# A four-mixer hybrid layer on one core: matmuls regrouped in the recurrent mixers, masks added once a bank, and attention products of two key tiles put together

## The chip, the cores and the metric

One core of one Trainium2 chip runs the whole program. The metric is the device time of one execution in microseconds, and the comparison is between medians of several executions. The engines are TensorE (PE for matmuls, PEld for weight loads), VectorE (DVE), ScalarE (ACT), GpSimd (POOL) and SyncE (SP), which issues most of the DMAs.

## The reference

Two layers over 1024 tokens of width 1024. Each layer projects the tokens into four groups of four heads of 64, mixes each group in another way, gates, projects back, adds to the scaled input and normalises:

```python
def hybrid_mixer(x, w_in, b_in, ...):
    cols = split_cols(jnp.einsum('btd,dn->btn', x, w_in) + b_in)
    # A: attention over a window of 128 keys, with a sink
    y_a = flat(banded_attention(q_a, k_a, heads(cols['a_v']), A_WINDOW, a_sinks)) * silu(cols['a_z'])
    # B: mLSTM in chunks of 128
    h_b = mlstm_chunkwise(q, k, v, i_pre, f_pre)
    y_b = sigmoid(cols['b_o']) * flat(h_b) * silu(cols['b_z'])
    # C: HGRN2, a gated recurrence
    o_c = hgrn2_chunkwise(heads(silu(cols['c_q'])), heads(log(f_c)), heads(1.0 - f_c), heads(cols['c_i']))
    y_c = flat(normed(o_c)) * silu(cols['c_z'])
    # D: compressed keys + 8 selected blocks of 64 + a window of 512
    o_d = nsa_attention(q_d, ...)
    y_d = flat(o_d) * silu(cols['d_z'])
    return jnp.einsum('btm,md->btd', concatenate([y_a, y_b, y_c, y_d], -1), w_out)

def reference(x, ...):
    h = layer_norm(x, ln0_g, ln0_b)
    for l in range(2):
        y = hybrid_mixer(h, ...)
        h = layer_norm(DN_ALPHA * h + y, ln_g[l], ln_b[l])
    return h
```

In the mLSTM of a chunk, with `b` the running sum of the log forget gates and `m` a running maximum:

```python
D = where(causal, b[t] - b[s] + i[s], -inf)
m_t = maximum(max(D, -1), b + m)
S = einsum('htd,hsd->hts', q, k) * exp(D - m_t)
num = S @ v + exp(b + m - m_t) * (q @ C)
```

## The kernel before, in words

The program is unrolled in Python. A stage is one half of the sequence (512 tokens, four tiles of 128) in one layer, so there are four stages. In each stage the four groups run in the order D, C, A, B. A group first makes its projections (`proj_tok`, `proj_feat`: fp32r matmuls of a high and a low part, three for each product) and then loops over its four tiles ("mix"). The driver at the end of the file runs one tile of the current group, then one projection of the next, and so on, so that projections stand between the mixers' matmuls. Within this order a scheduler fixes each engine's instruction order ahead of the run; the engines wait for each other by semaphores. Weights come as pieces by SP's DMA queue (`load_piece`), are rounded to a high part on ScalarE (L266), and POOL makes the low part (L267).

The pieces that the change touches:

- `scores` (L354) makes attention scores for one query tile. The keys are cut into one or two cuts of at most 512; a PSUM bank holds four heads of 128 keys, two of up to 256, or one of more. For each head: two fp32r score matmuls (L377, and L381 or L379), then for the first 128 keys of a full window a mask matmul (L383) and for the last 128 keys the causal mask (L385). A mask matmul multiplies a bf16 identity with a bf16 mask of 128 columns, so that 0 or -1e30 is added. VectorE takes the maximum of a bank (L387), ScalarE the exponential (L392); then the weights are scaled (L415, L417).
- `values` (L420) transposes the weights of one key tile for four heads (L427, four transposes into `ps_pt`, one of two PSUM buffers), copies them to an SBUF tile `PT` (ScalarE at odd tiles, L430, VectorE at even ones, L432; three buffers), and multiplies with the values (L434): for each pair of heads one fp32 matmul of 256 columns, into 64 of the 128 partitions of `O`. The next key tile follows. In D the compressed product (L672) comes before, into the same `O`.
- Group C (L817 on): `front(c)` makes the decay factors (POOL L761, L762; ScalarE L767; VectorE L778), the score matmuls (L796, L801) and the masked tile `Af`. Then, for each of four heads, the product with the state `St` (L831: 64 rows, 64 columns) and the product with the values (L832: 128 rows, 64 columns); then two transposes of the keys (L836), the copy `kh` (L838), and the state's update (L843, L849). `ms` (L856) is a sum over 64 rows with two halves of the array.
- Group B: the gates of all four tiles and heads lie as rows 32c + h. VectorE scans them into `rB`, `rU`, `rM`, `rE` (L977 to L991). `front(c)` adds the causal mask (L1008, bf16 identity) and, for each head, spreads one row of `rM` over 128 partitions by an fp32 matmul of four rows with `sel` (L1012). The query-key products (L1017) share the bank `SW`. In the same way `rE` is spread into `xb` (L1032).

Of the kernel before, what the change touches and what calls it, by code (L numbers as in the profile page):

```python
# [23 lines left out]
WB, AB, PB, PTB, PER_TILE = 6, 2, 6, 3, 1  # L24
# [65 lines left out]
def consts():  # L90
    c = {}
    c['ident'] = np.eye(128, dtype=np.float32)
    q = np.arange(128)
    lo = np.where(q[None, :] <= q[:, None], 0.0, NEG)
    up = np.where(q[None, :] > q[:, None], 0.0, NEG)
    c['masks'] = np.stack([lo, up, lo.T], 1).astype(np.float32)
# [29 lines left out]
    sel = np.zeros((128, 4, 128), np.float32)  # L126
    for h in range(4):
        sel[h::32, h, :] = 1.0
    c['sel'] = sel.reshape(128, 512)
    return c  # L130
# [15 lines left out]
def tile_hybrid(ctx, tc, I, out, dbg=None, depth=DEPTH):  # L146
# [74 lines left out]
    masks = const.tile([128, 3, 128], BF16, name="masks_bf")  # L221
    cmask = const.tile([128, NT, 64], BF16, name="cmask_bf")
    identb = const.tile([128, 128], BF16, name="ident_bf")
# [4 lines left out]
    sel = const.tile([128, 512], F32, name="sel_sb")  # L228
# [4 lines left out]
    G.tensor_copy(identb, ident)  # L233

    def load_consts():

        for name, dst in (('masks', masks), ('cmask', cmask), ('lvm', lvm)):
            d2 = dst.rearrange("p a b -> p (a b)")
            n = d2.shape[1]
            m_ = mp.tile([128, 512], F32, tag="P", name="m_", bufs=PB)  # L240
            SY.dma_start(m_[:, :n], I[name] if name == 'lvm' else I[name].rearrange("p a b -> p (a b)"))
            G.tensor_copy(d2, m_[:, :n])
        for name, dst in (('rowok', rowok), ('rope_e', rope_e), ('impk', impk), ('sel', sel)):
            SY.dma_start(dst, I[name])
# [109 lines left out]
    def scores(i, k0, A1, A2, kcols, Kblk, weigh, win, sink=None, A3=None):  # L354
# [10 lines left out]
        for c, (a, b) in enumerate(cuts):  # L365
            n = b - a
            hb = 4 if n <= 128 else 2 if n <= 256 else 1
            Pc = [mp.tile([128, 2, 512], F32, tag="P", name="P", bufs=PB) for _ in range(2)]
            P.append(Pc)
            for h0 in range(0, NH, hb):  # L370
                Sp = psS.tile([128, 512], F32, tag="S", name="S_ps")[:, :hb * n].rearrange("p (h k) -> p h k", h=hb)
                for z in range(hb):
                    h = h0 + z
                    o_ = Sp[:, z, :]
                    m0, m1 = lo_mask and c == 0, b == nk * 128
                    kc_ = kcols(h, a, b)
                    PE.matmul(o_, A1[:, h, :], kc_, start=True, stop=False)  # L377
                    if Kblk is not None:
                        PE.matmul(o_, A3[:, h, :], Kblk[:, a:b], start=False, stop=not (m0 or m1))  # L379
                    else:  # L380
                        PE.matmul(o_, A2[:, h, :], kc_, start=False, stop=not (m0 or m1))  # L381
                    if m0:
                        PE.matmul(o_[:, 0:128], identb, masks[:, 1, :], start=False, stop=not m1)  # L383
                    if m1:
                        PE.matmul(o_[:, n - 128:n], identb, masks[:, 0, :], start=False, stop=True)  # L385
# [33 lines left out]

    def values(sc, Vt, O, first, last):  # L420
        k0, cuts, P = sc
        nk = cuts[-1][1] // 128
        for c, (a, b) in enumerate(cuts):
            for kb in range(a // 128, b // 128):
                ps = psT.tile([128, 4, 128], F32, tag="T", name="ps_pt")
                for h in range(NH):
                    PE.transpose(ps[:, h, :], P[c][h // 2][:, h % 2, kb * 128 - a:kb * 128 - a + 128], ident)  # L427
# [3 lines left out]
                else:  # L431
                    V.tensor_copy(PT, ps)  # L432
                for g in range(2):
                    PE.matmul(O[64 * g:64 * g + 64, :], Vt(k0 + kb, g),  # L434
                              PT[:, 2 * g:2 * g + 2, :].rearrange("p a b -> p (a b)"),
                              start=(first and kb == 0), stop=(last and kb == nk - 1))
# [3 lines left out]
    def groups(stage):  # L440
# [83 lines left out]
        def group_D():  # L524
# [86 lines left out]
            def front(t):  # L611
# [8 lines left out]
                PE.matmul(Sc3, identb, bc(cmask[:, i, :nc_], 4, 0), start=True, stop=False)  # L620
# [76 lines left out]
        def group_C():  # L697
# [121 lines left out]
            for c in range(NTH):  # L819
# [4 lines left out]
                O = psO.tile([128, 256], F32, tag="O", name="Oc")  # L824
                for ct in range(2):
                    for hh in range(2):
                        h = 2 * ct + hh
                        rows = slice(64 * hh, 64 * hh + 64)
                        o_ = O[rows, ct * 128:(ct + 1) * 128]
                        if i > 0:  # L830
                            PE.matmul(o_, St[rows, ct, :], qe[rows, ct * 128:(ct + 1) * 128], start=(ct == 0), stop=False)  # L831
                        PE.matmul(o_, Vc[:, c, 64 * h:64 * h + 64], Af[:, hh, ct, :], start=(i == 0 and ct == 0), stop=(ct == 1))  # L832
                if i < NT - 1:
# [4 lines left out]
                    S.copy(out=kh.rearrange("p a b -> p (a b)"), in_=kt_ps)  # L838
                    s_ps = psT.tile([128, 2, 64], F32, tag="T", name="s_ps")
# [73 lines left out]
        def group_B():  # L913
# [55 lines left out]
            V.tensor_tensor(lf[:, 0, :].rearrange("p (c w) -> p c w", c=4)[:, :, 0:4], l1, l0, op=OP.subtract)  # L969
            V.tensor_copy(lf[:, 1, :].rearrange("p (c w) -> p c w", c=4)[:, :, 0:4], gi[:, :, 12:16])  # L970
# [5 lines left out]
            rk = sm.tile([128, 4], F32, tag="rk", name="rk")  # L976
            V.tensor_tensor_scan(rB, ones, r_ps[:, 0, :], 0.0, op0=OP.mult, op1=OP.add)  # L977
# [4 lines left out]
            if hf == 1:  # L982
                V.tensor_copy(rk[0:4, 0:1], mcar[0:4, :])
            for c in range(NTH):
                p_ = slice(32 * c, 32 * c + 4)
                dst = rk[32 * c + 32:32 * c + 36, 0:1] if c < NTH - 1 else mcar[0:4, :]
# [4 lines left out]
            V.tensor_scalar(rE, rM, rk[:, 0:1], None, op0=OP.add)  # L991
            u_ps = psT.tile([128, 2, 128], F32, tag="T", name="u_ps")
# [9 lines left out]
            def front(c):  # L1002
                i = T0 + c
                cs_ = slice(c * 128, (c + 1) * 128)
                p_ = slice(32 * c, 32 * c + 4)
                SW = [psS.tile([128, 512], F32, tag="S", name="SW") for _ in range(2)]
                for hh in range(2):
                    PE.matmul(SW[hh][:, 0:256].rearrange("p (h t) -> p h t", h=2), identb, bc(masks[:, 2, :], 2, 0),  # L1008
                              start=True, stop=False)
                    for ct in range(2):  # L1010
                        h = 2 * ct + hh
                        PE.matmul(SW[hh][:, ct * 128:(ct + 1) * 128], sel[p_, h * 128:(h + 1) * 128], rM[p_, :],  # L1012
                                  start=False, stop=(ct == 1))
# [17 lines left out]
                for p in range(2):  # L1031
                    PE.matmul(xb[:, p, :], sel[p_, 256 * p + 64:256 * p + 192], rE[p_, :], start=True, stop=True)  # L1032
# [177 lines left out]
```

## Time and profile before

| | |
|---|---|
| median of three runs | 1646.14 us (1645.08 to 1652.29) |
| the profiled execution | 1654.33 us; span 1652.5 us |
| instructions | 29596, of them 10948 matmul records |
| granted TensorE clock, mean | 0.962 |
| DMA | 126.70 MB, mean 77 GB/s |

A row of the busy times gives the time in which an engine had an instruction, as a share of the span; TensorE's matmuls are pipelined, so that the durations of neighbours overlap and the distance between two starts says more. Rows of the order of time give the start in us from the span's start, the duration, the engine, the line, the operation, out<-in, its rows*columns in the array, then partitions x elements, and a count where equal ones follow each other. Groups give the count, the busy time, the mean duration in ns and the idle time of the engine before them.

### The profile page before, as it was taken

The page shows a single profiled execution, that of the slowest core. Times are in us where ns is not written, and L with a number is a line of the kernel's source. Part 1 is how long each engine was busy: PE and PEld are TensorE (multiplying, and loading weights), DVE is VectorE, ACT ScalarE, POOL GpSimd, SP SyncE. Part 2 cuts the span into 40 slices and gives each one's busy share as a digit, 9 for nine tenths or more (in the row PEclk, how much of TensorE's full clock was granted, in tenths as well). Part 3 has the DMA queues.
Part 4 walks back from the last instruction along what each step waited for, and adds up shares of the span by engine and source line. Part 5 has one row for each costly group of instructions (what it writes and reads, how often), then busy time and mean ns, then how long its engine had stood idle before and what let it go on. Part 6 is the DMA issues. An engine that isn't in the chain of part 4 may idle for free.

```text
span 1652.5 us, 29596 instructions
## 1 busy us (share of the span) xinstructions
PE 1538.6 (93%) x10948; PEld 1206.1 (73%) x10948; DVE 1026.2 (62%) x2454; ACT 798.3 (48%) x1865; POOL 848.7 (51%) x1173
## 2 busy tenths in 40 slices
PE   4999999899979989999998999999997999999995
PEld 3787688678767657787877768786886765688774
DVE  6256835874787776357447676456448777735737
ACT  2356535544356664455435653444434666434541
POOL 4733784546643138634575468544565321873442
PEclk9999999989989999999999999999998999799997
DMA  5322023441441001224134212233134210022311
GB/s 180 91 64 59 15 76 90 155 142 45 120 144 52 26 1 46 65 68 142 44 108 153 74 33 56 55 107 105 36 105 160 55 52 1 20 66 65 90 52 51
DMA packets 64752, 126.70 MB, mean 77 GB/s; under 512 B 10112, under 2 KB 16032, under 8 KB 64608
## 3 DMA queue, kind: packets, MB, share of 16 engines
q1 hardware_dynamic: 63744, 122.72, 25.4%
q8 instruction: 86, 1.41, 0.4%
q10 hardware_dynamic: 864, 2.10, 0.3%
q14 instruction: 58, 0.48, 0.1%
HBM read 114.30 MB, written 10.49 MB: 76 GB/s over the span
## 4 chain that ended last, share of the span: by engine, by line
PE 66%; DVE 19%; POOL 5%; issue 3%; DMA 3%; ACT 3%; SPq 0%; DVEq 0%; POOLq 0%; ACTq 0%
PE ps_f L307 7%; PE ps_f L306 6%; PE ps_f L305 6%; PE ps_p L290 5%; PE ps_p L291 4%; PE ps_p L292 4%; PE ps_pt L427 4%; PE O L434 4%; PE ps_o L478 2%; PE ps_o L476 2%; PE S_ps L377 2%; DVE QK L950 2%; PE ps_o L477 2%; PE S_ab L796 2%; DMA w_raw<-in_w_in 2%
## 5 line engine op out<-in xcount | busy, mean ns | idle before, releaser
L267 POOL TENSOR_TENSOR w_split<-w_raw,w_split 128x512 fp32r<-128x512 f32 (+2 forms) x320 | 416.0, 1307 | 380.7 <-ACT w_split L266 350.6
L266 ACT CAST w_split<-w_raw 128x512 fp32r<-128x512 f32 (+2 forms) x320 | 194.4, 611 | 238.9 <-DMA w_raw<-in_w_in 109.5
L305 PE MATMUL ps_f<-hT_hi,w_split 128*128 128x512 f32 x608 | 246.0, 405 | 0.0
L306 PE MATMUL ps_f<-hT_lo,w_split 128*128 128x512 f32 x608 | 244.0, 401 | 0.0
L307 PE MATMUL ps_f<-hT_hi,w_split 128*128 128x512 f32 x608 | 243.5, 402 | 0.0
L290 PE MATMUL ps_p<-w_split,hT_hi 128*128 128x256 f32 (+1 forms) x768 | 227.3, 298 | 8.0 <-DVE hT_lo L257 5.5
L291 PE MATMUL ps_p<-w_split,hT_hi 128*128 128x256 f32 (+1 forms) x768 | 222.8, 291 | 0.0
L292 PE MATMUL ps_p<-w_split,hT_lo 128*128 128x256 f32 (+1 forms) x768 | 222.1, 290 | 0.0
L392 ACT ACTIVATE P<-S_ps,stt 128x256 f32<-128x256 f32 (+3 forms) x256 | 133.8, 530 | 91.7 <-DVE stt L387 49.7
L290 PEld LDWEIGHTS ps_p<-w_split,hT_hi 128*128 128x128 f32 x768 | 149.4, 195 | 14.1 <-DVE hT_lo L257 7.2
L291 PEld LDWEIGHTS ps_p<-w_split,hT_hi 128*128 128x128 f32 x768 | 149.6, 195 | 2.2 <-issue 1.2
L292 PEld LDWEIGHTS ps_p<-w_split,hT_lo 128*128 128x128 f32 x768 | 149.2, 194 | 1.8 <-issue 1.2
L307 PEld LDWEIGHTS ps_f<-hT_hi,w_split 128*128 128x128 f32 x608 | 115.4, 190 | 28.1 <-issue 2.8
L306 PEld LDWEIGHTS ps_f<-hT_lo,w_split 128*128 128x128 f32 x608 | 115.3, 190 | 26.3 <-issue 3.3
L305 PEld LDWEIGHTS ps_f<-hT_hi,w_split 128*128 128x128 f32 x608 | 115.5, 190 | 25.6 <-issue 1.9
L387 DVE TENSOR_REDUCE stt<-S_ps 128x1 f32<-128x384 f32 (+3 forms) x182 | 111.1, 625 | 28.4 <-PE S_ps L385 15.1
L476 PE MATMUL ps_o<-w_split,Y 128*128 128x512 f32 x256 | 114.7, 448 | 8.6 <-DVE acc L483 6.7
L427 PE MATMUL ps_pt<-ident_sb,P 128*128 128x128 f32 x648 | 103.3, 286 | 8.6 <-DVE P L417 8.6
L478 PE MATMUL ps_o<-w_split,Y 128*128 128x512 f32 x256 | 106.7, 425 | 1.5 <-POOL Y L462 1.3
L427 PEld LDWEIGHTS ps_pt<-ident_sb,P 128*128 128x128 f32 x648 | 71.3, 143 | 48.6 <-issue 41.3
L477 PE MATMUL ps_o<-w_split,Y 128*128 128x512 f32 x256 | 106.0, 414 | 0.0
L434 PE MATMUL O<-PT,Vd 128*64 128x256 f32 x528 | 86.8, 413 | 7.2 <-DVE PT L432 7.0
(351 smaller groups left out, 3258.5 us busy)
## 6 DMA issues: line engine op xcount, KB each, us to landing
w_raw<-in_w_in SPq DMA_DIRECT2D x224, 256.0 KB, 2.7
w_raw<-in_w_out SPq DMA_DIRECT2D x64, 256.0 KB, 2.6
w_raw<-in_w_in SPq DMA_DIRECT2D x16, 276.0 KB, 2.8
w<-in_w SPq DMA_DIRECT2D x8, 512.0 KB, 4.4
hs<-acc SPq DMA_DIRECT2D x8, 512.0 KB, 2.6
h_t<-hs SPq DMA_DIRECT2D x8, 512.0 KB, 4.4
acc<-hs SPq DMA_DIRECT2D x8, 512.0 KB, 4.2
out<-acc SPq DMA_DIRECT2D x7, 512.0 KB, 2.6
```

What stands on the lines that cost most here:

```text
L266: S.copy(out=hi, in_=raw_)
L267: G.tensor_tensor(lo, raw_, f(hi), op=OP.subtract)
L290: PE.matmul(ps[:, :n], a, hi, start=(k == 0), stop=False)
L291: PE.matmul(ps[:, :n], a, lo, start=False, stop=False)
L292: PE.matmul(ps[:, :n], b, hi, start=False, stop=(k == 7))
L305: PE.matmul(ps, a, x1, start=(k == 0), stop=False)
L306: PE.matmul(ps, a, x2, start=False, stop=False)
L307: PE.matmul(ps, b, x1, start=False, stop=(k == 7))
L427: PE.transpose(ps[:, h, :], P[c][h // 2][:, h % 2, kb * 128 - a:kb * 128 - a + 128], ident)
L434: PE.matmul(O[64 * g:64 * g + 64, :], Vt(k0 + kb, g), PT[:, 2 * g:2 * g + 2, :].rearrange("p a b -> p (a b)"), start=(first and kb == 0), ...
L476: PE.matmul(ps, a, hi, start=(k == 0), stop=False)
L478: PE.matmul(ps, b, hi, start=False, stop=(k == 1))
```

## The change

Five edits:

- `scores`: the mask is added once a bank, after all heads' score matmuls, by an fp32r identity and an fp32r mask that is read repeatedly for the heads. Where a bank has two masks over 256 keys (group A), one matmul of 512 columns adds both. The compressed mask (L620) and group B's (L1008) become fp32r as well.
- `values`: key tiles go in pairs. Both are transposed and copied; then both products stand together, the later tile's first, held in that order by an edge in the instruction order. `PT` gets a fourth buffer.
- Group C: the key transposes and `kh` come before the products; the four state products come first, then the four value products.
- Group B: the rows are split into two fp32r parts on rows 32c + h and 32c + 8 + h and spread over four columns of blocks in `RB` (VectorE); two heads' rows are then spread by one fp32r matmul of 128 rows and 256 columns, and `xb` by one as well.
- Constants: `sel` is twice as wide and is cast to fp32r on POOL; a small table `rowsel` is loaded besides.

```diff
+ISSUE = mybir.DependencyInfo(mybir.DependencyClass.NoSync, mybir.DependencyReason.DATA)
 # scores
                 for z in range(hb):
-                    PE.matmul(o_, A1[:, h, :], kc_, start=True, stop=False)
+                    PE.matmul(o_, A1[:, h, :], kc_, start=(z == 0), stop=False)
...
+                if m0 and m1 and n == 256:
+                    PE.matmul(Sp, identr, bc(masks[:, 0:2, :].rearrange("p a b -> p (a b)"), hb, 0), start=False, stop=True)
+                else:
                     if m0:
-                        PE.matmul(o_[:, 0:128], identb, masks[:, 1, :], start=False, stop=not m1)
+                        PE.matmul(Sp[:, :, 0:128], identr, bc(masks[:, 0, :], hb, 0), start=False, stop=not m1)
                     if m1:
-                        PE.matmul(o_[:, n - 128:n], identb, masks[:, 0, :], start=False, stop=True)
+                        PE.matmul(Sp[:, :, n - 128:n], identr, bc(masks[:, 1, :], hb, 0), start=False, stop=True)
 # values
+    def after(later, earlier):
+        tc.add_manual_dep(later.ins, earlier.ins.name, ISSUE, reason="order")
...
+        for g0 in range(0, nk, 2):
+            PTs = []
+            for kb in range(g0, min(g0 + 2, nk)):
                 (four transposes, copy to PT, as before)
+                PTs.append((kb, PT))
+            prev = None
+            for n_, (kb, PT) in enumerate(reversed(PTs)):
                 for g in range(2):
+                    mm = PE.matmul(O[64 * g:64 * g + 64, :], Vt(k0 + kb, g), PT[...], ...)
+                    if prev is not None:
+                        after(mm, prev)
+                    prev = mm
 # group C
-                for ct in range(2):
-                    for hh in range(2):
-                        if i > 0:
-                            PE.matmul(o_, St[rows, ct, :], qe[...], start=(ct == 0), stop=False)
-                        PE.matmul(o_, Vc[...], Af[:, hh, ct, :], start=(i == 0 and ct == 0), stop=(ct == 1))
                 if i < NT - 1:
                     (kt_ps transposes, kh copy)
+                if i > 0:
+                    for ct in range(2):
+                        for hh in range(2):
+                            PE.matmul(O[rows, ...], St[rows, ct, :], qe[...], start=(ct == 0), stop=False)
+                for ct in range(2):
+                    for hh in range(2):
+                        PE.matmul(O[...], Vc[...], Af[:, hh, ct, :], start=(i == 0 and ct == 0), stop=(ct == 1))
 # group B
+            RB = mp.tile([128, 6, 128], F32R, tag="RB", name="RB")
+            for src, j, n, tmp in ((rM, 0, 4, rk2[:, 0]), (rE, 4, 2, rk2[:, 1])):
+                V.tensor_copy(RH, src)
+                V.tensor_tensor(tmp, src, f(RH), op=OP.subtract)
+                V.tensor_scalar(tmp, tmp, rowsel[:, 1:2], None, op0=OP.mult)
+                V.scalar_tensor_tensor(tmp, f(RH), rowsel[:, 0:1], tmp, op0=OP.mult, op1=OP.add)
+                V.tensor_tensor(RB[:, j:j + n, :], bc(tmp, n, 0), rowsel[:, 2 + j:2 + j + n]..., op=OP.mult)
...
-                    for ct in range(2):
-                        PE.matmul(SW[hh][:, ct * 128:(ct + 1) * 128], sel[p_, h * 128:(h + 1) * 128], rM[p_, :], ...)
+                    PE.matmul(SW[hh][:, 0:256]..., sel[:, c * 128:(c + 1) * 128], RB[:, hh:4:2, :], start=False, stop=True)
...
-                for p in range(2):
-                    PE.matmul(xb[:, p, :], sel[p_, 256 * p + 64:256 * p + 192], rE[p_, :], start=True, stop=True)
+                PE.matmul(xb, sel[:, 512 + c * 128:512 + (c + 1) * 128], RB[:, 4:6, :], start=True, stop=True)
```

More of the change, by code (lines that the diff above doesn't have):

```diff
@@ L125, in consts @@
     c['lvm'] = np.stack(lv, 1).astype(np.float32).reshape(128, 448)
-    sel = np.zeros((128, 4, 128), np.float32)
+    r = np.arange(128)
+    sel = np.zeros((128, 2, 4, 128), np.float32)
     for h in range(4):
-        sel[h::32, h, :] = 1.0
-    c['sel'] = sel.reshape(128, 512)
+        for k in range(4):
+            for row in (32 * k + h, 32 * k + 8 + h):
+                sel[row, 0, k, :] = 1.0
+                sel[row, 1, k, 64 * (h % 2):64 * (h % 2) + 64] = 1.0
+    c['sel'] = sel.reshape(128, 1024)
+    part = [(r % 32 // 8 == z) & (r % 8 < 4) for z in range(2)]
+    own = (r[:, None] % 8 == np.arange(4)) & (part[0] | part[1])[:, None]
+    pair = (r[:, None] % 8 // 2 == np.arange(2)) & (part[0] | part[1])[:, None]
+    c['rowsel'] = np.concatenate([np.stack(part, 1), own, pair], 1).astype(np.float32)
     return c
@@ L220, in tile_hybrid @@
     sin = cload('sin', [128, NT, 32], S)
-    masks = const.tile([128, 3, 128], BF16, name="masks_bf")
-    cmask = const.tile([128, NT, 64], BF16, name="cmask_bf")
-    identb = const.tile([128, 128], BF16, name="ident_bf")
+    masks = const.tile([128, 3, 128], F32R, name="masks_r")
+    cmask = const.tile([128, NT, 64], F32R, name="cmask_r")
+    identr = const.tile([128, 128], F32R, name="ident_r")
     rowok = const.tile([128, 1], F32, name="rowok_sb")
@@ L227, in tile_hybrid @@
     lvm = const.tile([128, 7, 64], I8, name="lvm_i8")
-    sel = const.tile([128, 512], F32, name="sel_sb")
+    sel = const.tile([128, 1024], F32R, name="sel_sb")
+    rowsel = const.tile([128, 8], F32, name="rowsel_sb")
     ones = const.tile([128, 128], F32, name="ones")
@@ L232, in tile_hybrid @@
     G.memset(c_eps, C_EPS)
-    G.tensor_copy(identb, ident)
+    G.tensor_copy(identr, ident)
     def load_consts():
-        for name, dst in (('masks', masks), ('cmask', cmask), ('lvm', lvm)):
-            d2 = dst.rearrange("p a b -> p (a b)")
+        for name, dst in (('masks', masks), ('cmask', cmask), ('lvm', lvm), ('sel', sel)):
+            d2 = dst.rearrange("p a b -> p (a b)") if len(dst.shape) == 3 else dst
             n = d2.shape[1]
-            m_ = mp.tile([128, 512], F32, tag="P", name="m_", bufs=PB)
-            SY.dma_start(m_[:, :n], I[name] if name == 'lvm' else I[name].rearrange("p a b -> p (a b)"))
+            m_ = mp.tile([128, 1024], F32, tag="P", name="m_", bufs=PB)
+            SY.dma_start(m_[:, :n], I[name] if len(I[name].shape) == 2 else I[name].rearrange("p a b -> p (a b)"))
             G.tensor_copy(d2, m_[:, :n])
-        for name, dst in (('rowok', rowok), ('rope_e', rope_e), ('impk', impk), ('sel', sel)):
+        for name, dst in (('rowok', rowok), ('rope_e', rope_e), ('impk', impk), ('rowsel', rowsel)):
             SY.dma_start(dst, I[name])
@@ L422, in values @@
         nk = cuts[-1][1] // 128
-        for c, (a, b) in enumerate(cuts):
-            for kb in range(a // 128, b // 128):
+        where = [(c, kb * 128 - a) for c, (a, b) in enumerate(cuts) for kb in range(a // 128, b // 128)]
+        for g0 in range(0, nk, 2):
+            PTs = []
+            for kb in range(g0, min(g0 + 2, nk)):
+                c, o_ = where[kb]
                 ps = psT.tile([128, 4, 128], F32, tag="T", name="ps_pt")
                 for h in range(NH):
-                    PE.transpose(ps[:, h, :], P[c][h // 2][:, h % 2, kb * 128 - a:kb * 128 - a + 128], ident)
+                    PE.transpose(ps[:, h, :], P[c][h // 2][:, h % 2, o_:o_ + 128], ident)
                 PT = mp.tile([128, 4, 128], F32, tag="PT", name="PT", bufs=PTB)
@@ L432, in values @@
                     V.tensor_copy(PT, ps)
+                PTs.append((kb, PT))
+            prev = None
+            for n_, (kb, PT) in enumerate(reversed(PTs)):
                 for g in range(2):
-                    PE.matmul(O[64 * g:64 * g + 64, :], Vt(k0 + kb, g),
-                              PT[:, 2 * g:2 * g + 2, :].rearrange("p a b -> p (a b)"),
-                              start=(first and kb == 0), stop=(last and kb == nk - 1))
+                    mm = PE.matmul(O[64 * g:64 * g + 64, :], Vt(k0 + kb, g),
+                                   PT[:, 2 * g:2 * g + 2, :].rearrange("p a b -> p (a b)"),
+                                   start=(first and g0 == 0 and n_ == 0),
+                                   stop=(last and g0 + 2 >= nk and n_ == len(PTs) - 1))
+                    if prev is not None:
+                        after(mm, prev)
+                    prev = mm
     lay, hd = {}, {}
@@ L838, in group_C @@
                     S.copy(out=kh.rearrange("p a b -> p (a b)"), in_=kt_ps)
+                O = psO.tile([128, 256], F32, tag="O", name="Oc")
+                if i > 0:
+                    for ct in range(2):
+                        for hh in range(2):
+                            rows = slice(64 * hh, 64 * hh + 64)
+                            PE.matmul(O[rows, ct * 128:(ct + 1) * 128], St[rows, ct, :], qe[rows, ct * 128:(ct + 1) * 128],
+                                      start=(ct == 0), stop=False)
+                for ct in range(2):
+                    for hh in range(2):
+                        h = 2 * ct + hh
+                        PE.matmul(O[64 * hh:64 * hh + 64, ct * 128:(ct + 1) * 128], Vc[:, c, 64 * h:64 * h + 64], Af[:, hh, ct, :],
+                                  start=(i == 0 and ct == 0), stop=(ct == 1))
+                if i < NT - 1:
                     s_ps = psT.tile([128, 2, 64], F32, tag="T", name="s_ps")
```

42 lines of the change are left out of this document (20 added, 22 removed).

## The prediction, made before the changed kernel ran

> **What bounds the kernel now.** I read the busy times first, then the chain that ended last, then the engines by stage, and last the order of time on TensorE, because most of the change reorders matmuls.
>
> ```profile
> PE 1538.6 (93%) x10948; PEld 1206.1 (73%) x10948; DVE 1026.2 (62%) x2454; ACT 798.3 (48%) x1865; POOL 848.7 (51%) x1173
> PE 66%; DVE 19%; POOL 5%; issue 3%; DMA 3%; ACT 3%; SPq 0%; DVEq 0%; POOLq 0%; ACTq 0%
> ```
>
> TensorE is busy 93% of the 1652.5 us span, and 66% of the chain is TensorE's. So a microsecond of TensorE saved is worth at most one, and on average, by the chain, about 0.66. Two stretches show where that differs (columns: length; busy PE, PEld, DVE, ACT, POOL; granted clock; DMA): a C loop, then a D loop.
>
> ```profile
> 188.00:262.00 74.00, 71.58 (x775) 58.02 (x775) 35.86 (x111) 30.10 (x63) 58.61 (x98) 0.95 0.21 58
> 460.00:624.00 164.00, 152.23 (x981) 107.32 (x981) 125.21 (x318) 101.51 (x252) 51.84 (x70) 0.95 0.17 50
> ```
>
> TensorE is the fullest engine in both. The next one is POOL in C (58.61 of 74) and VectorE in D (125.21 of 164). These decide how much of a TensorE saving survives.
>
> A matmul's duration in these rows overlaps its neighbour's, so I price by the distance from one start to the next. An fp32 matmul that isn't a transpose stands as two instructions.
>
> **The change, part by part.**
>
> *Masks (score banks).* Before, each head gets a bf16 matmul of 128 columns for each mask: 280 in all.
>
> ```profile
> L385 PE MATMUL S_ps<-masks_bf,ident_bf 128*128 128x128 bf16 x192 | 43.9, 229 | 0.0
> L383 PE MATMUL S_ps<-masks_bf,ident_bf 128*128 128x128 bf16 x88 | 20.6, 234 | 0.0
> ```
>
> The order of time on TensorE, in D and then in A (columns: start, duration):
>
> ```profile
> 487.66 0.28 PE L379 MATMUL S_ps<-KD,A 80*128 80x256 f32 x1
> 487.78 0.23 PE L385 MATMUL S_ps<-masks_bf,ident_bf 128*128 128x128 bf16 x1
> 487.82 0.37 PE L377 MATMUL S_ps<-KD,A 128*128 128x256 f32 x1
> 488.03 0.28 PE L379 MATMUL S_ps<-KD,A 80*128 80x256 f32 x1
> ```
> ```profile
> 267.66 0.23 PE L383 MATMUL S_ps<-masks_bf,ident_bf 128*128 128x128 bf16 x1
> 267.72 0.22 PE L385 MATMUL S_ps<-masks_bf,ident_bf 128*128 128x128 bf16 x1
> 267.75 0.36 PE L377 MATMUL S_ps<-KA,A 128*128 128x256 f32 x1
> 267.96 0.40 PE L476 MATMUL ps_o<-w_split,Y 128*128 128x512 f32 x1
> ```
>
> From one L379 to the next is 0.37 us; the two score matmuls of 256 columns take 0.12 each (487.66 to 487.78), so a mask costs 0.13, most of it on the matmul behind it (0.21 instead of 0.12). A pair of masks (group A, 56 heads) costs 0.30 - 0.12 = 0.18. Before: 56 x 0.18 + 168 x 0.13 = 31.9 us. After, from the code's cuts: 88 banks of one head (128 columns) and 28 of two heads (256) at no more than the 0.12 of a 256-column matmul, and 34 of 512 columns at 0.23 (the distance of two L305-L307 rows below): 116 x 0.12 + 34 x 0.23 = 21.7. Saved: 10 us. The compressed scores' mask (16 matmuls) only swaps type; I take nothing for it.
>
> Of loading the identity, this:
>
> ```profile
> 1396.75 0.19 PEld L379 LDWEIGHTS S_ps<-KD,A 80*128 80x128 f32 x1
> 1397.20 0.10 PEld L385 LDWEIGHTS <-ident_bf 128*128 128x128 bf16 x1 [0.27 <-issue]
> ```
>
> A 4-byte weight load takes 0.19 against 0.10 for the bf16 identity. Were that 0.09 exposed at all 150 masks left, 13.5 us would be lost and the 10 saved would be a loss of 3.5; those are the ends for this part. I take the saving, since a 256-column matmul with a 4-byte weight starts 0.12 after its predecessor in the row at 487.66, with its 0.19 load behind the matmul before it. [...]
>
> *Attention values.* Before, each key tile's product stands alone between transposes or projections.
>
> ```profile
> 495.30 0.39 PE L306 MATMUL ps_f<-hT_lo,w_split 128*128 128x512 f32 x1
> 495.53 0.40 PE L307 MATMUL ps_f<-hT_hi,w_split 128*128 128x512 f32 x1
> 495.85 0.65 PE L434 MATMUL O<-PT,Vd 128*64 128x256 f32 x4
> 496.44 0.66 PE L427 MATMUL ps_pt<-ident_sb,P 128*128 128x128 f32 x4
> ```
> ```profile
> 489.05 1.08 PE L434 MATMUL O<-PT,Vd 128*64 128x256 f32 x8
> 490.06 1.09 PE L427 MATMUL ps_pt<-ident_sb,P 128*128 128x128 f32 x8
> ```
>
> L307 holds TensorE 0.32 ahead of a product instead of 0.23; one product takes 0.59 and two together 1.01, so the second costs 0.42. A run of products of any length thus costs 0.09 + 0.17 = 0.26 on top, as TensorE goes from 128 output columns to 64 and back. In order of time I count 162 such runs (L434 and L672), the first at 98.7 us and the last at 1561, 134 with one product and 20 with two. After the change there are 46 pairs or single tiles in each layer, 92 in all, and at most 16 runs of the compressed product beside them: 92 to 108. Saved 54 to 70 runs x 0.26; I take 60: 15.6 us. The first product of a pair now waits for the copy of the second tile, on ScalarE. TensorE has projections to run there, so I take nothing; without that cover it is the slower rival below. The fourth PT buffer moves nothing on a queue.
>
> *Group C (HGRN2).*
>
> ```profile
> 219.43 0.38 PE L831 MATMUL Oc<-qe,St 64*64 64x128 f32 x2
> ...
> 222.27 0.39 PE L290 MATMUL ps_p<-w_split,hT_hi 128*128 128x256 f32 x1
> ...
> 245.84 0.45 PE L843 MATMUL s_ps<-Vc,kh 128*64 128x64 f32 x8
> 246.22 0.65 PE L856 MATMUL ms<-sq,ones 64*64 64x256 f32 x4
> 246.80 0.50 PE L305 MATMUL ps_f<-hT_hi,w_split 128*128 128x512 f32 x1
> ```
>
> A chunk's eight products, L831 and L832 in turn and so alternating between two shapes, take 222.27 - 219.43 = 2.84 us. Afterwards four of one shape, in pairs on different rows and columns of the array, then four of the other. The first four stream as many columns as L856, which takes 0.58 for them with its switch; the second four half as many as the two products of 1.01 above, 0.42 + 0.17 = 0.59. With 0.09 for a switch: 1.26. Saved 1.58 a chunk, in 14 chunks (a sequence's first has no state): 22 us. Moving the kt transposes ahead takes their switch from between products and state update, to ahead of the products, and gives kh's copy on ScalarE cover: I take nothing for it. What is late next in C is POOL's E chain.
>
> [...]
>
> *Group B (mLSTM).*
>
> ```profile
> 777.88 1.15 PE L1012 MATMUL SW<-R,sel_sb 4*128 4x128 f32 x8
> 778.97 0.71 PE L1017 MATMUL SW<-QK 64*128 64x128 f32 x8
> ```
> ```profile
> 797.51 0.28 PE L1008 MATMUL SW<-masks_bf,ident_bf 128*128 128x256 bf16 x1
> 797.73 0.71 PE L1012 MATMUL SW<-R,sel_sb 4*128 4x128 f32 x4
> ```
>
> A chunk's row spreads cost 1.09 (eight instructions of four rows), two masks 0.22 each, and the four L1032 instructions, of L1012's shape, half of 1.09: 2.07 us. After: two masks, two spreads and one for xb, each 256 columns at 0.12: 0.60. Saved 1.47 in each of 16 chunks: 23.5 us. The QK products between them keep their two switches.
>
> Added on VectorE for each of four stages, ahead of the first spread: for each of two rows sets a copy, a subtraction, two scalings and a spread.
>
> ```profile
> L989 DVE SCALAR_TENSOR_TENSOR R<-R x4: 293/1292/1378, 347.7 to 1571.4; 128x128 f32<-128x128 f32 x4
> L990 DVE TENSOR_SCALAR R<-R x4: 215/218/2258, 349.1 to 1573.2; 128x128 f32<-128x128 f32 x4
> L483 DVE TENSOR_TENSOR acc<-acc,ps_o 128x512 f32<-128x512 f32 x96 | 65.1, 679 | 25.3 <-PE ps_o L478 24.6
> PE SW L1012 <- DVE R L990: 1.9, 1, 1.9
> ```
>
> The copy and one scaling go by L990's 0.22, the other two by the least of L989, 0.29, the spreads by L483: 2 x (0.22 + 0.29 + 0.22 + 0.29) + 0.68 + half of it = 3.1 us; at the slow ends of L989 and L990, where POOL works at the same time, some 8. TensorE waited for this chain in one stage of four (the last row), so 3 us come out exposed; at worst 8 in one and 3 in three, 17. The gates' second rows add one small VectorE and a POOL operation more, some 0.3 in the same chain, which I count in the 3. At the start SP's queue gets one transfer more (rowsel) and twice the bytes of sel ahead of the next weights, and POOL casts sel ahead of the weights' split; the first projections wait for VectorE's norm at that time, so I take 1 us.
>
> **The sum.** TensorE: 10 + 15.6 + 22 + 23.5 = 71 us. At the chain's 0.66: 47. Less 3 and 1: 43 us. The profiled execution took 1654.33 us, 1.8 over its span; 1654.3 - 43 = 1611. It stands 8.2 above the median of the runs, so on the median 1603.
>
> **Rivals.**
> 1. *POOL and VectorE take over.* In C a stage of 74 us with 58.61 of POOL loses 5.6 us of TensorE, in D 125.21 of VectorE stand under 152. If half of the 47 is given back to waits on E, on stt and on the weights' split: 1646 - 23 + 4 = 1627. For it: the chain is 34% elsewhere. Against: neither is over 80% of its stretch.
> 2. *Nearly all of it arrives.* 1646 - 71 + 4 = 1579. For it: TensorE at 93%, and its idle stretches are short.
> 3. *The regrouping doesn't pair.* Products of one shape follow each other but don't overlap (the two groups of 64 columns run in turn) in C: its 22 us fall to the switches alone, 7 x 0.09 x 14 = 9; with the identity's loads exposed as well (-3.5 for +10) TensorE saves 71 - 13 - 13.5 = 44.5, at 0.66 29: 1646 - 29 + 4 = 1621. Against it: the pairs in L856 and L434.
> 4. *Slower.* Both products of a pair wait for ScalarE's copy of the later tile:
>
> ```profile
> L430 ACT COPY PT<-ps_pt x70: 562/584/604, 120.1 to 1559.1; 128x512 f32<-128x512 f32 x70
> ```
>
> The copy takes 0.58 and stands behind exponentials in an engine that works in order. If each of 92 groups waits t, the loss is 92 t; from t = 0.47 us it eats the 43. At 0.6: 1646 + 55 - 43 = 1658. For it: in L434's waits the copies are already the cause (7.0 us in all). Against: before, that tile's product waited for the same copy.
>
> ```profile
> PE O L434 <- DVE PT L432: 7.0, 8, 3.1
> ```
>
> **How the numbers follow.** The forecast, 1603 with a range of its own of 1590 to 1616, 0.57; rival 1 0.17; rival 2 0.1; rival 3 0.1; rival 4 0.06. From 1578 (rival 2's middle) to 1630 (just beyond rivals 1 and 3) it holds 8 in 10, allowing for each case's own spread; 17 us of the row chain in place of 3 would bring the forecast to 1617, inside. A measurement here tells 0.5%, 8 us, from no change. Faster 0.89: all but rival 4 and a tail of rival 1; same 0.06; slower 0.05.
>
> **What would show it.** Right: L385's and L383's heirs down to 150 without a longer score matmul behind them; O products in runs of eight; Oc about 1.2 us a chunk in two blocks; the spreads and xb five matmuls of 256 columns; TensorE's busy time down by some 60. Wrong: new waits of O on PT's ScalarE copy, of the first spread on RB, or TensorE's idle time (span less busy, 114 us) rising by as much as was saved.

## The result, and the profile after

| | before | after |
|---|---|---|
| median time, first comparison | 1645.61 us | 1599.15 us, ratio 0.9711 [0.9676, 0.9746] |
| second and third comparison | 1644.25, 1646.37 us | 1597.66, 1600.10 us, ratios 0.9714 [0.9686, 0.9742] and 0.9714 [0.9691, 0.9737] |
| the profiled execution | 1654.33 us | 1595.67 us |
| span; granted clock | 1652.5 us; 0.962 | 1593.9 us; 0.966 |

The forecast was 1603. The page of the changed kernel, busy times and the chain that ended last:

```profile
PE 1468.0 (92%) x10674; PEld 1192.1 (75%) x10674; DVE 1051.9 (66%) x2494; ACT 795.2 (50%) x1865; POOL 852.5 (53%) x1182
PE 61%; DVE 19%; POOL 7%; DMA 5%; issue 4%; ACT 4%; SPq 0%; ACTq 0%; DVEq 0%; POOLq 0%
```

TensorE's busy time fell by 70.6 us and its time without work (span less busy) rose from 113.9 to 125.9. The four parts in the order of time on TensorE, group C first, then a pair of values in D, then group B:

```profile
684.16 0.65 PE L868 MATMUL Oc<-qe,St 64*64 64x128 f32 x8
684.74 0.66 PE L873 MATMUL Oc<-Af,Vc 128*64 128x128 f32 x8
685.33 0.51 PE L508 MATMUL ps_o<-w_split,Y 128*128 128x512 f32 x1
```
```profile
495.31 1.08 PE L462 MATMUL O<-PT,Vd 128*64 128x256 f32 x8
496.32 0.66 PE L357 MATMUL ps_q<-ident_sb,qd 128*128 128x128 f32 x4
```
```profile
789.87 0.37 PE L1056 MATMUL SW<-masks_r,ident_r 128*128 128x256 f32 x1
790.07 0.28 PE L1058 MATMUL SW<-RB,sel_sb 128*128 128x256 f32 x1
790.19 0.28 PE L1056 MATMUL SW<-masks_r,ident_r 128*128 128x256 f32 x1
790.31 0.28 PE L1058 MATMUL SW<-RB,sel_sb 128*128 128x256 f32 x1
790.51 0.71 PE L1063 MATMUL SW<-QK 64*128 64x128 f32 x8
```

The eight products of a chunk take 685.33 - 684.16 = 1.17 us (2.84 before; 1.26 predicted). A pair of value products takes 1.01, as the double run before did; runs of value products, of any length, are now 114 in place of 162. Two masks and two spreads take 0.64 (790.51 - 789.87). The masks, in the groups of the same kernel, are 144 in place of 280 here, with 6 of other shapes beside them:

```profile
L401 PE MATMUL S_ps<-masks_r,ident_r 128*128 128x128 f32 x56 | 12.5, 223 | 0.0
L396 PE MATMUL S_ps<-masks_r,ident_r 128*128 128x512 f32 x28 | 11.1, 395 | 0.0
L401 PE MATMUL S_ps<-masks_r,ident_r 128*128 128x256 f32 x28 | 8.0, 286 | 0.0
L399 PE MATMUL S_ps<-masks_r,ident_r 128*128 128x128 f32 x32 | 7.4, 233 | 0.0
```

The waits that the change could have made, from the waits and from the groups (last column: idle time before, and what ended it):

```profile
PE SW L1058 <- DVE RB L1039: 1.5, 1, 1.5
PE xb L1077 <- DVE RB L1039: 0.5, 1, 0.5
```
```profile
L462 PE MATMUL O<-PT,Vd 128*64 128x256 f32 x528 | 78.2, 406 | 5.0 <-DVE PT L457 3.1 <-ACT PT L455 1.7
L452 PE MATMUL ps_pt<-ident_sb,P 128*128 128x128 f32 x648 | 104.2, 288 | 14.8 <-DVE P L433 7.7 <-DVE PT L457 6.9
```

The row chain is exposed by 2.0 us (3 predicted). The copy on ScalarE, the slower rival's mechanism, costs 1.7 us in all. The last row holds a wait that the prediction did not have: the transposes stand 6.9 us for VectorE's copy out of `ps_pt`, which has two buffers only. The kernel before has no such wait, and the kernels without paired values have at most 0.6 us, on ScalarE's copy; the six profiles in which the pairs stay together have 6.7 to 7.6 us of it.

**Time at half clock.** The experiments cannot be read without the granted clock, so here is how it looks (order of time on TensorE, changed kernel, start of group D in the second stage):

```profile
453.66 0.39 PE L318 MATMUL ps_f<-hT_hi,w_split 128*128 128x512 f32 x1
460.58 0.66 PE L389 MATMUL S_ps<-KD,A 128*128 128x384 f32 x1 [6.53 <-DVE Pc L660]
...
463.06 0.41 PE L301 MATMUL ps_p<-w_split,hT_hi 128*128 128x256 f32 x1
463.27 0.41 PE L302 MATMUL ps_p<-w_split,hT_hi 128*128 128x256 f32 x1
...
465.31 0.28 PE L303 MATMUL ps_p<-w_split,hT_lo 128*128 128x256 f32 x1
465.43 0.28 PE L301 MATMUL ps_p<-w_split,hT_hi 128*128 128x256 f32 x1
```
```profile
460.50:464.60 4.10, 4.02 (x17) 4.05 (x18) 4.00 (x10) 3.50 (x8) 1.42 (x2) 0.50 0.71 249
464.60:468.00 3.40, 2.89 (x23) 2.68 (x23) 3.40 (x5) 1.85 (x5) 2.24 (x2) 0.99 0.52 172
```

TensorE waits 6.53 us; the clock (third number from the end of a window's row) is then 0.50, and the same projection matmuls start 0.21 us apart. At 464.6 the clock is full again and they start 0.12 apart. So a busy time holds two things: work at full clock, and the surplus of the time at half clock. The surplus is (1 - clock) x span, half of the time at half clock (124.9 us before, 108.6 after). What I call work below is busy time less that: 1538.6 - 0.038 x 1652.5 = 1475.8 before and 1468.0 - 0.034 x 1593.9 = 1413.8 after, 62.0 less.

This is an estimate: it takes half the clock for half the speed (the projections above start 0.21 us apart against 0.12) and counts all time at half clock as busy, and by the clock's records TensorE is idle in 13 to 26 us of it, depending on the kernel. With those left out, work is 1486.4 before and 1426.6 after, 59.8 less, and the differences between kernels below move by up to 5 us; where this matters the exact count is given beside the other.

### The profile page after: what moved, and what is told of

It reads as the page before. It is cut to its first block, busy times and chain, and to the rows that moved or that the text cites. A ratio compares the mean times of both kernels' runs of the same rounds, so it can differ in the third digit from the quotient of the medians.

```text
span 1593.9 us, 29110 instructions
## 1 busy us (share of the span) xinstructions
PE 1468.0 (92%) x10674; PEld 1192.1 (75%) x10674; DVE 1051.9 (66%) x2494; ACT 795.2 (50%) x1865; POOL 852.5 (53%) x1182
## 4 chain that ended last, share of the span: by engine, by line
PE 61%; DVE 19%; POOL 7%; DMA 5%; issue 4%; ACT 4%; SPq 0%; ACTq 0%; DVEq 0%; POOLq 0%
PE ps_f L316 7%; PE ps_f L317 6%; PE ps_f L318 6%; PE ps_p L301 5%; PE ps_p L302 4%; PE ps_p L303 4%; PE ps_pt L452 4%; PE O L462 3%; DMA w_raw<-in_w_in 3%; PE S_ps L389 2%; PE ps_o L510 2%; PE ps_o L508 2%; DVE QK L987 2%; DVE acc L515 2%; PE ps_o L509 2%
## 5 line engine op out<-in xcount | busy, mean ns | idle before, releaser
L301 PE MATMUL ps_p<-w_split,hT_hi 128*128 128x256 f32 (+1 forms) x768 | 226.7, 297 | 12.1 <-DVE hT_lo L268 8.0
L508 PE MATMUL ps_o<-w_split,Y 128*128 128x512 f32 x256 | 110.9, 433 | 6.9 <-DVE acc L515 2.7
L452 PEld LDWEIGHTS ps_pt<-ident_sb,P 128*128 128x128 f32 x648 | 75.0, 146 | 45.8 <-issue 26.9
L510 PE MATMUL ps_o<-w_split,Y 128*128 128x512 f32 x256 | 104.7, 417 | 3.8 <-POOL Y L494 3.6
L509 PE MATMUL ps_o<-w_split,Y 128*128 128x512 f32 x256 | 103.8, 406 | 0.0
L389 PE MATMUL S_ps<-KD,A 128*128 128x384 f32 (+3 forms) x192 | 66.2, 369 | 20.3 <-DVE Pc L660 13.1
```

What stands on the lines that cost most here:

```text
L301: PE.matmul(ps[:, :n], a, hi, start=(k == 0), stop=False)
L452: PE.transpose(ps[:, h, :], P[c][h // 2][:, h % 2, o_:o_ + 128], ident)
L508: PE.matmul(ps, a, hi, start=(k == 0), stop=False)
L509: PE.matmul(ps, a, lo, start=False, stop=False)
L510: PE.matmul(ps, b, hi, start=False, stop=(k == 1))
```

## The experiments

All in one table. The clock is the mean over a kernel's timed runs, work is from its profile.

| kernel | time, us | ratio to before [95%] | clock | work, us |
|---|---|---|---|---|
| before (three comparisons) | 1644.45, 1644.25, 1646.37 | 1 | 0.9696, 0.9687, 0.9686 | 1475.8 |
| p_masks | 1645.50 | 1.0016 [0.9997, 1.0034] | 0.9594 | 1463.8 |
| p_values | 1657.27 | 1.0072 [1.0044, 1.0100] | 0.9560 | 1461.6 |
| p_groupC | 1635.61 | 0.9934 [0.9911, 0.9956] | 0.9633 | 1455.5 |
| p_groupB | 1626.04 | 0.9882 [0.9859, 0.9904] | 0.9728 | 1456.7 |
| w_only_CB | 1607.74 | 0.9768 [0.9748, 0.9787] | 0.9708 | 1439.5 |
| w_no_values | 1593.26 | 0.9673 [0.9643, 0.9704] | 0.9738 | 1422.8 |
| w2_no_values | 1591.77 | 0.9673 [0.9653, 0.9693] | 0.9728 | 1421.6 |
| r_after | 1597.66 | 0.9714 [0.9686, 0.9742] | 0.9656 | 1414.1 |
| r2_after | 1600.10 | 0.9714 [0.9691, 0.9737] | 0.9637 | 1414.6 |
| w_earlier | 1595.53 | 0.9703 [0.9675, 0.9732] | 0.9718 | 1427.9 |
| w_halves | 1599.49 | 0.9713 [0.9674, 0.9751] | 0.9675 | 1419.6 |
| w_mask_bf16 | 1605.50 | 0.9767 [0.9742, 0.9793] | 0.9624 | 1416.9 |

### Each part alone

**p_masks**: before, with the score masks added once a bank in fp32r (and the compressed mask in fp32r).

```diff
-                        PE.matmul(o_[:, 0:128], identb, masks[:, 1, :], start=False, stop=not m1)
+                    PE.matmul(Sp[:, :, 0:128], identr, bc(masks[:, 0, :], hb, 0), start=False, stop=not m1)
```

> The kernel before with the mask edit of the score banks alone (fp32r identity, once a bank; group B keeps its bf16 mask). Theory: 280 mask matmuls of 0.13 (0.18 a pair) become 150 of 0.12 to 0.23; TensorE saves 8 to 10 us, of which 0.66 arrive: 6 us faster, 1640. Rival (the 4-byte identity's loads are exposed): up to 2 us slower, 1648. A second rival: the order of instructions changes with any edit, and by itself moves the time by more than this.

**p_values**: before, with the key tiles in pairs, the later first, and four PT buffers.

```diff
-            for kb in range(nk):
+            for g0 in range(0, nk, 2):
+            ... for n_, (kb, PT) in enumerate(reversed(PTs)):
```

> The kernel before with the pairing of key tiles alone (fourth PT buffer included). Theory: 162 runs of O products become 111 in the fixed order; 51 x 0.26 us = 13 us of TensorE, 0.66 of it arrives: 9 us faster, 1637. Rival (both products of a pair wait for ScalarE's copy): TensorE idles ahead of L434's products by more than the 7 us of before, and the time is unchanged or longer, 1646 or more.

**p_groupC**: before, with group C's key transposes ahead and its products in two blocks.

```diff
-                        if i > 0: (state product)
-                        (value product)
+                if i > 0: (four state products)
+                (four value products)
```

> The kernel before with group C's regrouping alone. Theory: a chunk's eight products take 1.26 us in place of 2.84; TensorE saves 22 us; in C's stretches TensorE holds most of the chain, so 0.66 to 0.85 arrive: 15 to 19 us faster, 1628. Rival (POOL's exponent differences take over in C): half, 1635. [...]

**p_groupB**: before, with RB, two spreads and one xb matmul a chunk.

```diff
-                        PE.matmul(SW[hh][...], sel[p_, h * 128:(h + 1) * 128], rM[p_, :], ...)
+                    PE.matmul(SW[hh][...], sel[:, c * 128:(c + 1) * 128], RB[:, hh:4:2, :], ...)
```

> The kernel before with group B's spreads (and its mask and the new constants) alone. Theory: TensorE saves 19 to 23 us, 0.5 to 0.66 of it arrives, less 3 us for the longer row chain on VectorE and 1 at the start: 8 to 11 us faster, 1636. Rival (the longer row chain is exposed in all four stages, 3.1 us and more each): no gain, 1644 to 1648. If the four parts alone add up to the 46.5 us of the whole, the gain is TensorE time by part; if they add up to much less, the parts need each other; if more, they share a limit.

In time, only group B did better than its theory. Group C came out at its rival's number, the masks saved nothing, and the pairing was a loss of 13 us. The four changes add up to -13 us by these medians (-15 by the means), where the whole gives -46. Their pages, busy times, in the order of the table:

```profile
PE 1522.8 (93%) x10818; PEld 1212.0 (74%) x10818; DVE 1029.8 (63%) x2454; ACT 795.7 (49%) x1865; POOL 848.0 (52%) x1175
```
```profile
PE 1531.1 (93%) x10948; PEld 1214.0 (73%) x10948; DVE 1033.1 (62%) x2454; ACT 799.5 (48%) x1865; POOL 844.0 (51%) x1173
```
```profile
PE 1507.6 (93%) x10948; PEld 1191.7 (73%) x10948; DVE 1027.7 (63%) x2454; ACT 793.9 (49%) x1865; POOL 848.8 (52%) x1173
```
```profile
PE 1502.2 (92%) x10804; PEld 1184.5 (73%) x10804; DVE 1048.9 (65%) x2494; ACT 794.5 (49%) x1865; POOL 853.9 (53%) x1184
```

With the profiles' clocks (0.964, 0.958, 0.968, 0.972) the work saved is 12.0, 14.2, 20.3 and 19.1 us: 65.6 in all, and the whole change saves 62.0 (exactly counted 12.1, 13.4, 20.5 and 21.3: 67.3, and the whole 59.8). So the parts roughly add up in work, to 6 to 13% more than the whole. What does not add up is the surplus of the half clock: masks alone had 0.0102 less clock than the kernel before on the same chip, some 17 us of a 1643 us span, pairing 0.0136 less, 22 us, and group C 0.0063 less, 10 us; group B had 0.0032 more. Among the nineteen runs of before on that chip, whose instruction order is one and the same, 0.01 of clock goes with 12 us of time, a little under the 16 that the surplus would give. This shows that the two go together; that the clock is the price and not a by-product of waiting is argued, not shown.

p_masks fits its second rival, if the lower clock is the doing of the new order of instructions: the 17 us at half clock are more than the 12 us of saved work. The time of p_values lies on its rival's side (1646 or more), and the rival's wait is there, but too small for 13 us of time and 14 of saved work:

```profile
L447 PE MATMUL O<-PT,Vd 128*64 128x256 f32 x528 | 79.9, 416 | 9.0 <-ACT PT L440 5.7 <-DVE PT L442 3.1
```

The kernel before has 7.2 us in this place, 7.0 of it on VectorE's copy. No theory or rival of the four had the clock in its sum.

### The parts in company

**r_after**, **r2_after**: the changed kernel, unedited.

> The whole change once more, on the chip and beside the runs that the kernels below share. Theory (the parts add up in TensorE work at full clock, and what their separate times lack is idle time and time at half clock): about 1599 us, 45 us under the kernel before, at a granted clock near 0.965. Rival (the parts' separate times add up, and the first comparison flattered the whole): the sum of the four parts alone is -15 us, so 1629.

> The whole change, as the comparison for the three others: 1598 us within 3, granted clock 0.965 to 0.967. Theory and rivals agree here.

**w_no_values**, **w2_no_values**: the changed kernel with `values` as before.

```diff
-            for g0 in range(0, nk, 2):
-            ... for n_, (kb, PT) in enumerate(reversed(PTs)):
+            for kb in range(nk):
```

> The changed kernel with the attention values as before: one key tile at a time, three PT buffers, no edge in the order; masks, group C and group B stay changed. Theory (pairing saves TensorE work wherever it stands): the runs of O products go from 114 to about 155, TensorE's slots at full clock rise by 10 to 14 us, time 1607 to 1612. Rival (pairing is a loss by itself, as it was alone, +12 us): 1587, faster than the whole change.

> The changed kernel with attention values by single key tiles, again, beside the changed kernel itself on one chip. Theory (pairing saves some 9 us of TensorE work and pays as much or more in time at half clock): a granted clock 0.005 to 0.009 above the changed kernel's, and a time 1 to 7 us below it. Rival (the first comparison was chance; pairing is worth its work): equal clocks and a time 5 to 9 us above.

**w_only_CB**: the same, with the bf16 masks for each head (and the compressed mask in bf16) as well.

> Groups B and C regrouped, score masks for each head in bf16 and attention values by single key tiles as before. Theory (the parts add up in TensorE work at full clock; the masks' 12 us of it are saved also here): above the kernel without paired values (1593) by 8 to 14 us, 1601 to 1607, with a granted clock of 0.97 or more. Rival 1 (the masks save nothing in time, as they did alone): 1593. Rival 2 (times of the parts alone add up: -9 and -18): 1617.

The whole stands at 1598 to 1600 again, so the additive reading of times (1629) is out; in r2_after the clock, 0.9637, is a little under the 0.965 to 0.967 expected. w_only_CB is 16 us above the kernel without paired values beside it (1591.8), just outside its theory (8 to 14), and far from both rivals (1593, 1617). Now one part at a time, from the kernel before to w_only_CB and on: groups B and C together save 36.3 us of work (exactly counted 40) and 39 us of time; the masks, nothing by themselves, save 18 of work (exactly counted 13) and 16 of time beside them; the pairing saves 7 to 9 more of work (exactly counted 5 to 7) and loses time: 4.4 us in one comparison and 8.3 in the other. That is 0.3 and 0.5%, and in the first the intervals of the two ratios overlap; in the second they just touch. In the first of these two runs the runs of products rose to 155 and the work by 9, as its theory said, but the time went against it; the second, written after it, came out near its theory, with 8.3 us for 1 to 7. The two kernels' busy times and clocks, without and with pairing:

```profile
PE 1466.1 (92%) x10674; PEld 1180.8 (74%) x10674; DVE 1053.8 (66%) x2494; ACT 790.9 (50%) x1865; POOL 853.2 (54%) x1182
```
```profile
core 0: 1588.8 us, clock 0.972
```
```profile
PE 1470.6 (92%) x10674; PEld 1197.0 (75%) x10674; DVE 1051.5 (66%) x2494; ACT 794.6 (50%) x1865; POOL 852.0 (53%) x1182
```
```profile
core 0: 1600.6 us, clock 0.965
```

The paired kernel has the larger busy time with the smaller work. Over the timed runs its clock is 0.008 to 0.009 lower, 13 to 15 us of surplus, which is more than the 8 saved. Idle time has a share too: in these two profiles span less busy is 122.7 without pairing and 130.0 with it, and the wait for `ps_pt` is one of the new pieces. Over the three profiles with pairing and the two without, cut at each group's first score matmul, pairing saves 6 us of work (exactly counted) and costs 6 of surplus and 5 of idle time.

Where: not in the loops that hold most of the values, but behind them. In the same profiles the four stretches of group D are 6 us shorter with pairing, in all, and those of group C 9 us longer. Stretches with pairing (the changed kernel's first profile), then without: group B of the first stage from its first product with the values to the same output projection, group D of the third stage, and group C of the third stage.

```profile
358.00:439.10 81.10, 78.54 (x530) 66.67 (x530) 38.29 (x107) 31.02 (x73) 49.95 (x82) 0.93 0.24 69
...
834.60:960.40 125.80, 120.34 (x695) 95.85 (x693) 89.27 (x199) 77.01 (x183) 64.85 (x79) 0.97 0.32 93
...
960.40:1046.20 85.80, 81.12 (x934) 66.48 (x934) 51.65 (x137) 34.34 (x70) 68.58 (x118) 0.96 0.22 56
```
```profile
363.80:434.50 70.70, 68.50 (x512) 59.22 (x511) 38.26 (x103) 28.47 (x68) 47.30 (x78) 1.00 0.25 69
...
828.80:959.10 130.30, 124.72 (x709) 97.57 (x707) 93.53 (x205) 77.94 (x184) 68.61 (x87) 0.97 0.31 92
...
959.10:1038.30 79.20, 76.80 (x916) 62.47 (x915) 47.50 (x131) 32.83 (x70) 64.75 (x110) 0.98 0.23 58
```

In group B, 18 matmuls more and a clock of 0.93 in place of 1.00: 10.4 us longer. The 18 are projections that ran ahead of B's first product without pairing, so part of the 10.4 is only moved: from B's first matmul (317.1 with pairing, 318.1 without) to the next stage's first score matmul (421.9, 417.4) the difference is 5.5 us. In group C, 18 matmuls more and 6.6 us longer; they are products, transposes and output projections of group D's end, and D is 4.5 us shorter without them, so 2.1 us are left. Why just this order falls to half clock more often is not isolated: it would take the same order with the clock held, and no kernel here does that.

**w_earlier**: the changed kernel with the earlier tile's product first.

```diff
-            for n_, (kb, PT) in enumerate(reversed(PTs)):
+            for n_, (kb, PT) in enumerate(PTs):
```

> The changed kernel, but of a pair the earlier key tile's product comes first. Theory (the later tile's first keeps the pair together; otherwise the scheduler puts the first product ahead of the second tile's transposes, and the pair falls apart): about 159 runs of O products instead of 114, 45 x 0.26 = 12 us more TensorE work, time 1606 to 1611. Rival (the order of the two has no bearing on the time, since other work fills in): 1599 within 4 us.

The pairs fall apart as the theory said: 159 runs of products instead of 114, and 14 us more work (1427.9 against 1414). The time, though, is 1595.5, within the rival's bounds, at a clock of 0.9718. Again less pairing goes with more clock, and no time is lost by it.

### The other two disputes

**w_halves**: group C's blocks with the halves outside and the pairs inside.

```diff
-                    for ct in range(2):
-                        for hh in range(2):
+                    for hh in range(2):
+                        for ct in range(2):
```

> The changed kernel, but in group C the two products of one half of the array follow each other, in the state products and in the value products, so that only the middle two of four can lie beside each other. Theory (products on different halves overlap): each block of four takes three steps of 0.21 us instead of two, 30 blocks, Oc's slots 19.6 to about 26 us, time 3 to 6 us above the whole change. Rival (nothing overlaps; the saving in group C is only fewer switches of shape): Oc's slots stay within 1 us of 19.6 and the time does not move.

```profile
642.36 0.65 PE L868 MATMUL Oc<-qe,St 64*64 64x128 f32 x8
642.94 0.67 PE L873 MATMUL Oc<-Af,Vc 128*64 128x128 f32 x8
643.53 0.39 PE L301 MATMUL ps_p<-w_split,hT_hi 128*128 128x256 f32 x1
```

The block takes 1.17 us in this order too (643.53 - 642.36), and the time does not move. The theory's 6 us were wrong; the kernel's work is 5 us above the whole change's, but not in these blocks. In both orders the eight instructions of a block start about 0.055 us apart on average; the two of a lone product are 0.11 apart (at 219.43 in the kernel before). So they do run two at a time, and the edit did not take that away; it does not tell how much of group C's saving is overlap and how much is fewer switches of shape.

**w_mask_bf16**: the changed kernel with bf16 masks and identity for the score banks.

```diff
-                        PE.matmul(Sp[:, :, n - 128:n], identr, bc(masks[:, 1, :], hb, 0), ...)
+                        PE.matmul(Sp[:, :, n - 128:n], identb, bc(maskb[:, 1, :], hb, 0), ...)
```

> The changed kernel with one mask matmul a bank as there, but bf16 mask and bf16 identity for the score banks. Theory (in these rows a 4-byte identity's load is hidden behind the matmul before it, and a change of type costs on the matmul behind): score matmuls and masks together rise from 110 us of slots by 5 to 13, time 1600 to 1608. Rival (a 4-byte weight load of 0.19 against 0.10 us is exposed at every mask): the slots fall by up to 150 x 0.09 = 13 us, time 1589 to 1595.

Two of its groups of masks, beside the L401 and L396 rows of the changed kernel above (223 ns for 128 columns, 395 for 512):

```profile
L406 PE MATMUL S_ps<-masks_bf,ident_bf 128*128 128x128 bf16 x56 | 12.9, 231 | 0.0
...
L401 PE MATMUL S_ps<-masks_bf,ident_bf 128*128 128x512 bf16 x28 | 11.5, 409 | 0.0
```

From start to start, score matmuls and masks take 108.6 us in all, against 109.6 to 110.5 in the three profiles of the changed kernel. So neither side is right: no 13 us of exposed loads come back, and no 5 to 13 are added. The time, 1605.5, lies in the theory's range, but not for its reason: it is 5 to 8 us longer than the changed kernel's, at 2.5 us more work and 0.001 to 0.003 less clock (2 to 5 us); what brings these about is open, but it is not the masks' own time.

## Why the prediction was right or wrong

The number was right, 1603 against 1599, but partly by luck: three of its four terms were right as TensorE work, one was not worth its price, and the way from work to time was wrong.

- **Masks, 10 us**: 12 of work alone, 13 to 18 beside groups B and C. Right in kind. The identity's load is hidden, as the row at 487.66 said: going back to bf16 gave back 1 us of slots, not 13. The loads themselves took 0.19 us in fp32r (L401 in the changed kernel) and 0.10 in bf16 (L385 before); a loss of 3.5, the other end of this part, did not come.
- **Values, 15.6 us**: this is the step that failed. The runs fell to 114, not to 92 to 108, and the work by 14 alone and by 5 to 9 in company. I turned that into a gain of 10 us of time; it is a loss of 13 alone and of 4 to 8 in company. The wait that I named as the danger stayed small (1.7 to 3.1 us in the three profiles); one that I did not count came, 6.9 us on the two buffers of `ps_pt`, and the rest of the price is paid at half clock and in idle time, mostly behind group D. The row that I showed for the danger names VectorE's copy (L432), not ScalarE's.
- **Group C, 22 us**: 1.17 us a chunk for 1.26, 20.3 of work. Right as work; alone it gave only 9 us of time. The products of two halves go into one tile, `Oc`, and run two at a time: in the block at 684.16 the two of a pair start 0.01 apart, the pairs 0.11 to 0.16, and the eight state instructions take 0.58.
- **Group B, 23.5 us**: 19.1 of work (exactly counted 21). Two masks and two spreads cost 0.64 where I had 0.48: the first and the last of them, next to another shape, take 0.20 each instead of 0.12. VectorE's chain was exposed by 2.0 of the predicted 3 (4.1 in p_groupB).
- **The factor 0.66**: groups B and C give 39 us of time for 36 to 40 of work, the masks 16 for 13 to 18. In both the clock moves by only 0.002, and the price of a microsecond of work is about 1. The chain's share is no price: it was multiplied into the sum and made it 24 us too small.
- **What made up for it**: at a price of 1 the sum would have given 1579, which was rival 2. From there, 9 us less work was saved than summed (62 for 71), TensorE's idle time grew by 12 where 4 were foreseen, and the surplus at half clock by some 5 (51 us before at 0.9687, 56 after at 0.965): 1579 + 9 + 8 + 5 = 1601. This is an estimate, good to some 5 us: the idle time is from one profile each, and the two other profiles of the changed kernel have 130.6 and 130.0 where the first has 125.9. The factor of 0.66 stood in for these three without a reason, and that it hit their sum is luck. That idle time would rise was among the signs that I named for a wrong prediction; it rose by a sixth to a quarter of what was saved.

## What to carry to other kernels

Split TensorE's busy time into work and the surplus of the half clock before pricing a change; here the work of the parts added up and the time did not, and a part that looked worthless alone (masks) was worth its work in company. The chain's share was no price for saved matmul work in this kernel, with TensorE at 93%. And time a part by leaving it out of the whole: the version without paired values, 1592 to 1593 us, beats both kernels, the changed one by 0.3 to 0.5%.

## What the runs showed of the hardware

In the clock records of the kernel before and of the changed one the clock is full or half, and a stretch of either lasts 3.41 us or a multiple of it: 3.4 to 249.2 us in 37 stretches before, 3.4 to 235.5 in 35 after. Half clock also follows stretches in which TensorE was never idle. Group B's spreads as before, in p_groupC, windows and order of time:

```profile
1127.10:1130.50 3.40, 3.40 (x29) 2.59 (x29) 0.07 (x1) 1.29 (x5) 1.67 (x2) 1.00 0.43 104
1130.50:1137.30 6.80, 6.80 (x20) 5.29 (x21) 1.62 (x4) 4.00 (x10) 1.60 (x5) 0.51 0.07 27
```
```profile
1127.95 1.15 PE L1017 MATMUL SW<-R,sel_sb 4*128 4x128 f32 x8
1129.03 0.71 PE L1022 MATMUL SW<-QK 64*128 64x128 f32 x8
```

TensorE is busy for all of 1127.1 to 1130.5, but much of it with matmuls of 4 and 64 rows, and the next 6.8 us are at half clock. I divided the fourteen profiles into steps of 3.41 us, 6473 of them, and weighted TensorE's time by the share of the array that each matmul's rows and columns use. From full clock, 109 of 117 steps under 0.25 were followed by half clock, 116 of 486 between 0.25 and 0.55, and 4 of 5481 above. From half clock, all 151 steps above 0.9 were followed by full clock, and 5 of 92 under 0.6. Steps without idle time that were followed by half clock were 13, all in group B of the four kernels that still spread by four rows (two in the kernel before, from 1145.3 and from 1602.7 us), none in the ten that spread by 128: a gain of the change, if a small one, that the prediction did not have. Among steps without idle time the rows in use separate better than the share of the array: of 22 with under 0.6 of the rows in use, all in those four kernels, 13 were followed by half clock, and of 4670 with more, none. Another 115 had under 0.55 of the array in use and kept full clock; in 107 of these it was columns that were missing, and the rows stood above 0.6.
